# Second experts: eight places of 32 slots, weights of small places as whole rows, a new order of places

## The chip, the cores and the metric

The kernel runs on one core of one Trainium2 chip. The metric is the device time of one execution in microseconds (us). Each core has TensorE (PE; PEld is its weight load), VectorE (DVE), ScalarE (ACT), GpSimd (POOL) and SyncE (SP, which here only issues DMA), and 16 DMA engines.

## What is computed

Two transformer blocks run one after the other on 512 tokens of 1024 numbers, in float32. Each is a mixer and a mixture of experts. The change concerns the experts of the second block alone: 32 experts, of which a router picks 4 for every token. Cut to what matters:

```python
def moe_ffn(h, w_router, b_router, w_gu, b_gu, w_dn, b_dn):   # h: 512 x 1024
    logits = h @ w_router + b_router
    top_logits, top_e = lax.top_k(logits, 4)
    top_w = softmax(top_logits)
    ...                                    # tokens sorted by expert, blocks of one expert
    def expert_block(xe, e):
        gu = xe @ w_gu[e] + b_gu[e]        # 1024 -> 2048
        x_glu = minimum(gu[:, :1024], 7.0)
        x_lin = clip(gu[:, 1024:], -7.0, 7.0)
        act = (x_lin + 1) * (x_glu * sigmoid(1.702 * x_glu))
        return act @ w_dn[e] + b_dn[e]     # 1024 -> 1024
    ...                                    # y[token] += top_w * expert_block(...)
```

An expert's weights are 8 MiB for gate and up (w_gu, 1024 rows of 2048 numbers) and 4 MiB for down (w_dn): 12.58 MB, all of which are read for every expert that has a token. 512 x 4 = 2048 token-expert pairs are spread unevenly over the 32 experts.

## The kernel before

`moe2` (L2093) runs the second experts through `experts` (L1202), which lays out 32 **places**, one for each expert. Places 0 and 1 hold fixed experts; the others are filled on the chip by rank: `plan` (L838) sorts the experts by their number of tokens. Ranks are dealt to places by table: `PAIRS` names two places that have a second block of 64 slots beside 128 (a **pair**, for the two largest), and `SLOTS` names the places of 96 slots and of 64; all others have 128. Before, the places read, with A for 128 slots, M for 96, S for 64 and P for a pair: `AAASMSMSSMMSPSMSMSSMPMSASSSSSSSS`. The last eight are all S. A token that finds no slot is taken by `overflow` (L883), which counts extra blocks; they run in a loop behind the places (L1354), as often as that count says.

**Weights.** Every place takes 12 pieces of 1 MiB, in the order of the list `seq` (L1217): four gate/up pieces of the first half of the 1024 inner columns (hf = 0), the previous place's two down pieces of its second half, four gate/up pieces of hf = 1, two down pieces of hf = 0. A gate/up piece (`src_of`, L2105) is 128 partitions x 4 rows x 512 columns, so each partition reads four runs of 2 KB, and neighbouring partitions lie 64 KB apart. A down piece is 128 partitions x 2 rows x 1024 columns, one run of 8 KB a partition. Nine buffers (`wraw`, L97) hold them; SP issues the load of piece i when piece i - 9 has been used (`free`, L1296).

**Products.** Places of 128 and 96 slots, and pairs, split each weight piece into two parts (`split`, L112: `whi` on ACT L117, `wlo` on DVE L118) and take three products for each (`mm_block`); a pair puts the second block's work into the same stream. A place of 64 slots (`col`) multiplies the raw piece in fp32 with no split, and two such products of 64 rows stand **side by side** in one 128-row PSUM tile (`col_gu` L1031 for gate beside up, `col_dn` L1045 for the two halves of the 1024 output columns). The bias enters as one more product, of a selector `bsel` that POOL makes for each place (`bias_of`, L2121) with the table of biases. The activation (`act`, L1057 to 1080) works on one half at a time: `ea` and `eb` from PSUM, Silu on ACT, the multiply L1080 on DVE for a 64-slot place, on POOL otherwise; `act_turn` (L1084) transposes on TensorE into `pt`, and `act_split` (L1090) copies out `ah`.

**Lists and rows of tokens.** For each place POOL makes one-hots (`oh`, `list_hot` L926) from the plan; TensorE sums them up (`list_sum` L929, into `pt`), DVE turns the sum into indices (`list_end`), and POOL gathers the token rows (`x_gather` L992, `xg` from U) and at the end adds the weighted result to Y by an indirect DMA (`y_scatter`, L1128 to 1140, `eo`, whose operands come from ACT L1139 and DVE L1134).

**Order.** The program is in a hand-written order: step i of the loop at L1310 multiplies piece i of `seq`, and hooks put the other work at steps relative to that (`at`, `LEAD`): one-hots 17 steps ahead of a place's first piece, list sum 14, list end 13, gather 12, transposes of the tokens 4 and 2 steps ahead; act at 2 to 5 steps behind a half's last gate/up piece; the scatter 2 steps behind its last down piece. Each engine does its instructions in this order.

## Time and profile before

| what | us |
|---|---|
| time before, median of 3 runs (2493.81 to 2495.08) | 2494.42 |
| the profiled execution | 2502.25 |
| its span (first to last instruction) | 2500.4 |
| second experts in that span, from about | 1300 |
| to about | 2465 |
| busy in these 1165 us: TensorE | 1106.63 |
| DVE, ACT, POOL | 583.86, 450.06, 308.16 |
| moved there by DMA | 409.75 MB |

The mean granted TensorE clock of the profiled execution was 0.955 of full speed (2.4 GHz). How the views are read: a row of **windows** gives the window from:to in us, its length, then busy us and number of instructions of PE, PEld, DVE, ACT and POOL in that order, the granted TensorE clock (1 is full), the mean busy share of the 16 DMA engines (overlaps count, so it can exceed 1), and GB/s. A row of **waits** is: who waited, on what, then total us, times, longest. A row of **groups** is: line, engine, operation, out<-in with shapes and count | busy us, mean ns of one | idle of that engine just before, and what ended most of it. A row of the **timeline** is start us, duration us, engine, line, operation, and in brackets the idle time before it with its releaser.

### The profile page before, as it was taken

To read this page: it belongs to the slowest core of one execution; us is meant where nothing else is said; L and a number is where in the kernel's file an instruction comes from. 1 tells how busy PE (TensorE), PEld (TensorE's weight loads), DVE (VectorE), ACT (ScalarE), POOL (GpSimd) and SP (SyncE) were. 2 spreads that over 40 slices of the span, in tenths; PEclk is the share of its full clock that TensorE was granted. 3 is DMA by queue.
4 is the path that set the end of the run, shared out by engine and by line. 5 is a ranking of instruction groups with operands and counts; after the bars stand their busy time and mean duration, and the time that the engine had idled before them with its cause. 6 is when DMAs were issued, how large, how long until landed. Compare 5 with 4: busy or idle time off the path is not lost. (4 is left out here: it accounts for less than half of the span.)

```text
span 2500.4 us, 32116 instructions
## 1 busy us (share of the span) xinstructions
PE 2287.3 (91%) x11341; PEld 1447.2 (58%) x11341; DVE 1420.5 (57%) x2710; ACT 1051.0 (42%) x1605; POOL 593.7 (24%) x596
## 2 busy tenths in 40 slices
PE   6999977998978999999969999999999999998984
PEld 2655656774647886778747655455555467543331
DVE  5454698875638756544578655475456367531112
ACT  3333446865525445532347444354344256421001
POOL 2001134534313020000243222162322133131111
PEclk9999988999989999999979999999999999999997
DMA  8767538988976135223578999999799998999997
GB/s 283 234 201 245 177 127 320 378 305 304 335 265 180 57 80 159 60 89 93 185 286 298 336 390 381 392 357 339 254 360 389 381 336 257 324 379 391 389 394 229
DMA packets 264678, 683.78 MB, mean 273 GB/s; under 512 B 21260, under 2 KB 61028, under 8 KB 235840
## 3 DMA queue, kind: packets, MB, share of 16 engines
q1 hardware_dynamic: 240576, 607.88, 66.8%
q0 software_dynamic: 23648, 72.74, 11.0%
q8 instruction: 92, 1.51, 0.2%
q10 hardware_dynamic: 288, 1.05, 0.1%
q14 instruction: 74, 0.61, 0.1%
HBM read 643.74 MB, written 37.95 MB: 273 GB/s over the span
## 5 line engine op out<-in xcount | busy, mean ns | idle before, releaser
L118 DVE TENSOR_TENSOR wlo<-wraw,whi 128x1024 fp32r<-128x1024 f32 (+1 forms) x559 | 677.1, 1238 | 310.3 <-ACT whi L117 298.9
L117 ACT ACTIVATE whi<-wraw 128x1024 fp32r<-128x1024 f32 (+1 forms) x559 | 573.7, 1053 | 314.9 <-PE pm L80 120.8
L80 PE MATMUL pm<-wraw,xh 128*64 128x512 f32 x1280 | 321.9, 600 | 24.5 <-DMA wraw<-in_w_gu 24.3
L80 PE MATMUL pm<-whi,xh 128*128 128x512 f32 (+1 forms) x736 | 304.4, 414 | 3.4 <-ACT whi L117 3.4
L80 PE MATMUL pm<-wlo,xh 128*128 128x512 f32 (+1 forms) x736 | 291.7, 399 | 4.8 <-DVE wlo L118 4.8
L80 PE MATMUL pm<-whi,xl 128*128 128x512 f32 (+1 forms) x640 | 255.0, 399 | 0.0
L1140 POOL DMA_INDIRECT Y<-eo,isc x52 | 107.8, 2072 | 615.0 <-ACT eo L1139 232.4
L80 PEld LDWEIGHTS pm<-wraw,xh 128*64 128x64 f32 x1280 | 95.5, 137 | 208.2 <-issue 150.7
L1073 DVE TENSOR_SCALAR ea<-pm 64x512 f32<-64x512 f32 (+2 forms) x64 | 43.5, 680 | 235.1 <-PE pm L80 235.1
L80 PEld LDWEIGHTS pm<-whi,xh 128*128 128x128 f32 (+1 forms) x736 | 132.1, 179 | 59.7 <-issue 13.7
L80 PE MATMUL po<-wraw,ah 128*64 128x512 f32 x640 | 153.2, 601 | 0.1
L80 PEld LDWEIGHTS pm<-wlo,xh 128*128 128x128 f32 (+1 forms) x736 | 127.0, 172 | 41.0 <-DVE wlo L118 7.1
L992 POOL DMA_INDIRECT xg<-U,ig x52 | 88.6, 1704 | 226.4 <-issue 99.7
L926 POOL TENSOR_SCALAR oh<-slots,plan 128x64 bf16<-128x64 f32 (+2 forms) x168 | 139.1, 1051 | 0.4
L80 PEld LDWEIGHTS pm<-whi,xl 128*128 128x128 f32 (+1 forms) x640 | 113.8, 178 | 36.7 <-issue 0.6
L80 PE MATMUL po<-whi,ah 128*128 128x512 f32 (+1 forms) x320 | 132.5, 414 | 0.0
L80 PE MATMUL po<-whi,al 128*128 128x512 f32 (+1 forms) x320 | 128.1, 400 | 0.9 <-DVE al L1107 0.9
L80 PE MATMUL po<-wlo,ah 128*128 128x512 f32 (+1 forms) x320 | 128.2, 401 | 0.0
L1095 ACT ACTIVATE ah<-pt 128x256 f32<-128x256 f32 x40 | 15.4, 384 | 209.7 <-PE pt L1088 209.6
L1076 ACT ACTIVATE ea<-ea 64x512 f32<-64x512 f32 (+2 forms) x68 | 42.7, 628 | 140.7 <-DVE ea L1073 129.2
L80 PEld LDWEIGHTS po<-wraw,ah 128*64 128x64 f32 x640 | 51.3, 138 | 85.9 <-issue 80.1
L1080 POOL TENSOR_TENSOR eb<-eb,ea 96x512 f32<-96x512 f32 (+2 forms) x32 | 43.9, 1373 | 213.5 <-ACT ea L1076 153.5
(611 smaller groups left out, 4094.6 us busy)
## 6 DMA issues: line engine op xcount, KB each, us to landing
wraw<-in_w_gu SPq DMA_DIRECT2D x254, 1024.0 KB
wraw<-in_w_dn SPq DMA_DIRECT2D x127, 1024.0 KB
wraw<-in_w_e_down SPq DMA_DIRECT2D x32, 1024.0 KB
wraw<-in_w_e_up SPq DMA_DIRECT2D x31, 1024.0 KB
wraw<-in_w_e_gate SPq DMA_DIRECT2D x30, 1024.0 KB
wraw<-in_w_in SPq DMA_DIRECT2D x58, 512.0 KB
mz<-in_w_ada SPq DMA_DIRECT2D x80, 256.0 KB
wraw<-in_w_mod SPq DMA_DIRECT2D x26, 512.0 KB
```

Source lines behind the costliest of these rows:

```text
L80: self.nc.tensor.matmul(out, lhsT, rhs, start=start, stop=stop)
L117: nc.scalar.activation(h, v, AF.Copy)
L118: nc.vector.tensor_sub(l, v, h.bitcast(F32))
L926: (eng or self.nc.gpsimd).tensor_scalar(oh[:, c, :], self.slots[:, 0:n], poscol(c), None, op0=OP.is_equal)
L992: self.nc.gpsimd.indirect_dma_start(out=B.xg[0:B.n, :], out_offset=None, in_=self.U, in_offset=bass.IndirectOffsetOnAxis(ap=B.ig[:, :1], a ...
L1073: ve.tensor_scalar(a, g, 7.0, None, op0=OP.min)
L1076: nc.scalar.activation(a, a, AF.Silu, scale=1.702)
L1080: (nc.vector if B.col else nc.gpsimd).tensor_mul(B.b, B.b, B.a)
L1095: nc.scalar.activation(B.ah[hf], B.at.rearrange("p (k q) -> p k q", k=4), AF.Copy, scale=1.0 / 1.702 if B.bias else 1.0)
L1140: nc.gpsimd.indirect_dma_start(out=self.Y[:, :], out_offset=bass.IndirectOffsetOnAxis(ap=B.isc[:, :1], axis=0), in_=o, in_offset=None, com ...
```

## The change

Places of the second experts get a fourth size, and a new order: with X for 32 slots, `AAXMSMSPXXMSASMSPXXMSMSMXSMAXSSX`. There are 8 M, 10 S and 8 X (before 8 M and 18 S); the pairs stand at 7 and 16. In S and X places (**row** places)

- a gate/up piece is 128 partitions x 1 row x all 2048 columns: one run of 8 KB a partition, partitions 64 KB apart as before. `row_gu` multiplies gate and up of both halves from it; in an X place four products of 32 rows stand side by side in one PSUM tile (gate and up, two halves), in an S place two tiles hold two each (both halves of gate, both of up);
- both halves are activated at once (`row_act`, `row_turn`, `row_split`) on 2 x slots rows;
- all four down pieces follow behind the next place's first four gate/up pieces, so `seq` of a row place is eight gate/up pieces with the earlier place's four down pieces between the fourth and the fifth, and the scatter follows later. In an X place the down products stand four side by side too, and `y_scatter` adds two of them (ACT copy, then DVE multiply-add, for each half of the columns).

In all places the selector `bsel` has two halves of 128 rows (POOL: two operations of 128x128 for M, A and P where there was one, two of 128x64 for S and X as before for S), and the bias product goes over 128 rows. The first block's experts keep their tables and path.

```diff
-PAIRS = {2: (12, 20), 1: (6, 11)}
+PAIRS = {2: (7, 16), 1: (6, 11)}
...
+SLOTS = {2: ((3, 5, 10, 14, 19, 21, 23, 26),
+             (4, 6, 11, 13, 15, 20, 22, 25, 29, 30),
+             (2, 8, 9, 17, 18, 24, 28, 31)),
...
+    def row_gu(self, B, k, v):
+        n = B.n
+        if k == 0:
+            if B.col == 2:
+                B.pg = [self.pm.tile([128, 512], F32, name="pm") for _ in range(2)]
+            else:
+                p = self.pm.tile([128, 512], F32, name="pm")
+                B.pg = [p[0:64], p[64:128]]
+            for s in range(2):
+                for hf in range(2):
+                    B.bias("gu", B.pg[s][n * hf:n * hf + n], s, hf, True)
+        for s in range(2):
+            for hf in range(2):
+                c0 = 1024 * s + 512 * hf
+                self.mm(B.pg[s][n * hf:n * hf + n], B.xf[:, k, 0:n], v[:, 0, c0:c0 + 512], False, k == 7)
+    def row_dn(self, B, hf, jj, v):
+        n = B.n
+        if hf == 0 and jj == 0:
+            p = self.px.tile([128, 512], F32, name="po", tag="px")
+            B.po = [p[n * i:n * i + n] for i in range(B.col)]
+            for s in range(2):
+                B.bias("dn", B.po[s], s, 0, True)
+        for q in range(2):
+            for s in range(2):
+                i = s + 2 * q if B.col == 4 else s
+                self.mm(B.po[i], B.ah[hf][:, 2 * jj + q, :], v[:, q, 512 * s:512 * s + 512],
+                        hf == 0 and jj == 0 and i > 1, hf == 1 and jj == 1 and (q == 1 or B.col == 4))
+    def row_act(self, B, stage):
+        nc, ea, m = self.nc, self.ea, 2 * B.n
+        if stage == 0:
+            a = B.a = ea.tile([128, 512], F32, name="ea")[0:m]
+            b = B.b = ea.tile([128, 512], F32, name="eb")[0:m]
+            nc.vector.tensor_scalar(a, B.pg[0], 7.0, None, op0=OP.min)
+            nc.scalar.activation(a, a, AF.Silu, scale=1.702)
+            nc.vector.tensor_scalar(b, B.pg[1], 8.0, -6.0, op0=OP.min, op1=OP.max)
+        else:
+            nc.vector.tensor_mul(B.b, B.b, B.a)
+    def row_turn(self, B):
+        m = 2 * B.n
+        B.at = self.pt.tile([128, 512], F32, name="pt")[:, 0:4 * m]
+        for j in range(4):
+            self.nc.tensor.transpose(B.at[:, j * m:j * m + m], B.b[:, j:512:4], self.ident[0:m, 0:m])
+    def row_split(self, B):
+        m = 2 * B.n
+        ah = self.ea.tile([128, 4, 128], F32R, name="ah").bitcast(F32)[:, :, 0:m]
+        self.nc.scalar.activation(ah, B.at.rearrange("p (k q) -> p k q", k=4), AF.Copy, scale=1.0 / 1.702)
+        B.ah = [ah[:, :, 0:B.n], ah[:, :, B.n:m]]
...
-            (nc.vector if B.col else nc.gpsimd).tensor_mul(B.b, B.b, B.a)
+            nc.gpsimd.tensor_mul(B.b, B.b, B.a)
...
-            if B.col and s:
+            if B.col == 4:
+                nc.scalar.activation(d, B.po[s], AF.Copy, scale=B.w)
+                nc.vector.scalar_tensor_tensor(d, B.po[2 + s], B.w, d, op0=OP.mult, op1=OP.add)
+            elif B.col and s:
...
-        places = [[self.new_block(None, a > 0, 64 if a else size.get(b, 128), a > 0, size.get(b) == 64)
+        places = [[self.new_block(None, a > 0, 64 if a else size.get(b, 128), a > 0, {64: 2, 32: 4}.get(size.get(b), 0))
                    for a in range(2 if b in pairs else 1)] for b in range(E)]
+        rows = [nh == 2 and places[b][0].col > 0 for b in range(E)]
...
-                seq += [(b - 1, "dn", nh - 1, 0, jj) for jj in range(2)]
+                seq += [(b - 1, "dn", hf, 0, jj) for hf in range(0 if rows[b - 1] else nh - 1, nh) for jj in range(2)]
...
-                seq += [(b, "dn", 0, 0, jj) for jj in range(2)]
+                if not rows[b]:
+                    seq += [(b, "dn", 0, 0, jj) for jj in range(2)]
...
+            if rows[b]:
+                B, end = places[b][0], where[b, "gu", 1][-1]
+                for i, f in enumerate(((self.row_act, B, 0), (self.row_act, B, 1), (self.row_turn, B),
+                                       (self.row_split, B))):
+                    at(end + 1 if b == E - 1 else end + (1, 2, 4, 4.5)[i], *f)
+                at(where[b, "dn", 1][-1] + 2, self.y_scatter, B)
+                continue
...
+                    v = src[b]("row", 0, 0, 4 * hf + 2 * kk + s) if rows[b] else src[b]("gu", s, hf, kk)
+                raws[i] = self.raw(v, eng)
...
+                        if rows[b]:
+                            if q == 0 and what == "gu":
+                                self.row_gu(B, 4 * hf + 2 * kk + s, raws.pop(i))
+                            elif q == 0:
+                                self.row_dn(B, hf, s, raws.pop(i))
+                            else:
+                                free(i)
+                            continue
...
+                if what == "row":
+                    return w.rearrange("(p k) f -> p k f", k=8)[:, kk:kk + 1, :]
...
-        def bias_of(e, ef=None, col=False):
-            s_ = self.esm.tile([128, 128], F32R, name="bsel", bufs=4)
-            for d, v in ((s_[:, 0:64], ehalf[:, 0:1]), (s_[:, 64:128], ehalf[:, 1:2])) if col else ((s_, esel),):
-                nc.gpsimd.tensor_scalar(d, v.to_broadcast([128, d.shape[1]]), float(e) if ef is None else ef, None,
-                                        op0=OP.is_equal)
+        def bias_of(e, ef=None, col=0):
+            s_ = self.esm.tile([128, 2, 128], F32R, name="bsel", bufs=4)
+            for s in range(2):
+                nc.gpsimd.tensor_scalar(s_[:, s, 0:64 if col else 128],
+                                        ehalf[:, s:s + 1].to_broadcast([128, 64 if col else 128]),
+                                        float(e) if ef is None else ef, None, op0=OP.is_equal)
 
             def f(what, ps, s, hf, start):
-                c0, r = 512 * hf if what == "gu" else 1024, slice(64 * s, 64 * s + 64)
-                if col:
-                    self.mm(ps, s_[:, r].bitcast(F32), bias[:, c0:c0 + 512].bitcast(F32), start, False)
-                else:
-                    self.mm(ps, s_[r, 0:ps.shape[0]], bias[r, c0:c0 + 512], start, False)
+                c0 = 512 * hf if what == "gu" else 1024
+                l, r = s_[:, s, 0:ps.shape[0]], bias[:, c0:c0 + 512]
+                self.mm(ps, l.bitcast(F32) if col else l, r.bitcast(F32) if col else r, start, False)
```

The order on **PE at the end of the program**, where the last two places stand (there S and S, now S and X). `pm` are gate/up sums, `po` down sums, `xh` the tokens, `ah` the activated values, `wraw` the weight pieces; one row here is a run of equal instructions, a fp32 product counts once. Before, from the second half of place 30 on:

```order
L80 MATMUL po<-biasr,bsel 64x512 x2
L80 MATMUL po<-wraw,ah 64x512 x8
L80 MATMUL pm<-biasr,bsel 64x512 x2
L80 MATMUL pm<-wraw,xh 64x512 x8
L1088 MATMUL pt<-ident,eb 128x64 x4
L80 MATMUL pm<-wraw,xh 64x512 x8
L80 MATMUL po<-wraw,ah 64x512 x8
L80 MATMUL pm<-biasr,bsel 64x512 x2
L80 MATMUL pm<-wraw,xh 64x512 x8
L1088 MATMUL pt<-ident,eb 128x64 x4
L80 MATMUL pm<-wraw,xh 64x512 x8
L80 MATMUL po<-biasr,bsel 64x512 x2
```

Now, from the last gate/up products of place 30 (64 slots) to the end of place 31 (32 slots):

```order
L81 MATMUL pm<-wraw,xh 64x512 x8
L81 MATMUL pm<-biasr,bsel 32x512 x4
L81 MATMUL pm<-wraw,xh 32x512 x12
L1102 MATMUL pt<-ident,eb 128x128 x4
L81 MATMUL pm<-wraw,xh 32x512 x4
L81 MATMUL po<-biasr,bsel 64x512 x2
L81 MATMUL po<-wraw,ah 64x512 x16
L81 MATMUL pm<-wraw,xh 32x512 x16
L1102 MATMUL pt<-ident,eb 128x64 x4
L81 MATMUL po<-biasr,bsel 32x512 x2
L81 MATMUL po<-wraw,ah 32x512 x16
```

A place has one group of four transposes where it had two, its 16 down products stand in one row behind half of the next place's gate/up products, and in the last place they stand directly behind its transposes.

The order on **POOL in a 96-slot place that follows a 64-slot place**: `oh` are the one-hots, `eb` the multiply of the activation, `Y` the scatter of the place before, `xg` the gather. Before, at place 9:

```order
L1080 TENSOR_TENSOR eb<-eb,ea 96x512
L1140 DMA Y_114<-eo,isc 640x1024
L2124 TENSOR_SCALAR bsel<-ehalf,plan 128x64 x2
L926 TENSOR_SCALAR oh<-slots,plan 128x64 x4
L1080 TENSOR_TENSOR eb<-eb,ea 96x512
L992 DMA xg<-U_112,ig 64x1024
```

Now, at place 21:

```order
L1133 TENSOR_TENSOR eb<-eb,ea 96x512
L2204 TENSOR_SCALAR bsel<-ehalf,plan 128x128 x2
L927 TENSOR_SCALAR oh<-slots,plan 128x96 x4
L1196 DMA Y_114<-eo,isc 640x1024
L993 DMA xg<-U_112,ig 96x1024
L1133 TENSOR_TENSOR eb<-eb,ea 96x512
```

The scatter stands behind selector and one-hots now, where it stood ahead of them.

## Rows read from the trace of the kernel before

**Rows 1.** The page: busy time of each engine, share of the span, instructions.
```profile
PE 2287.3 (91%) x11341; PEld 1447.2 (58%) x11341; DVE 1420.5 (57%) x2710; ACT 1051.0 (42%) x1605; POOL 593.7 (24%) x596
```

**Rows 2.** Windows in the second experts: busy us (count), clock, DMA share, GB/s.
```profile
1300.00:2465.00 1165.00, 1106.63 (x4847) 604.24 (x4845) 583.86 (x787) 450.06 (x581) 308.16 (x286) 0.98 0.97 352
1300.00:1400.00 100.00, 94.53 (x419) 73.65 (x419) 82.19 (x92) 67.38 (x77) 43.33 (x32) 0.97 0.90 308
1425.00:1630.00 205.00, 196.35 (x869) 103.64 (x866) 111.96 (x165) 85.46 (x109) 45.78 (x44) 0.98 1.04 387
1630.00:1860.00 230.00, 220.38 (x963) 129.33 (x963) 132.24 (x172) 102.03 (x130) 83.35 (x64) 0.97 0.92 323
2020.00:2160.00 140.00, 138.44 (x592) 89.56 (x594) 86.99 (x99) 70.07 (x86) 40.41 (x35) 0.97 0.83 276
2261.00:2430.00 169.00, 150.31 (x640) 56.31 (x638) 27.42 (x59) 16.80 (x35) 21.64 (x33) 1.00 1.04 391
```

**Rows 3.** Windows cut at single places: 96 slots, 64, a pair, 64.
```profile
1646.00:1685.00 39.00, 39.00 (x178) 26.14 (x178) 33.07 (x43) 26.02 (x30) 26.97 (x16) 1.00 1.02 348
1685.00:1715.00 30.00, 30.00 (x145) 13.46 (x145) 12.29 (x17) 10.43 (x16) 4.01 (x7) 1.00 0.91 325
1715.00:1775.00 60.00, 60.00 (x255) 40.17 (x256) 32.90 (x41) 25.39 (x33) 20.64 (x16) 1.00 0.81 292
2295.00:2328.00 33.00, 29.69 (x129) 11.12 (x127) 5.64 (x13) 3.36 (x7) 4.95 (x8) 1.00 1.04 393
```

**Rows 4.** DMA view: 1300:2465, then 2306.5:2311 (2 KB), then 2369:2373.6 (mostly 8 KB).
```profile
DMA packets 153355, 409.75 MB, mean 352 GB/s; under 512 B 6962, under 2 KB 6962, under 8 KB 137330
DMA packets 873, 1.75 MB, mean 389 GB/s; under 512 B 25, under 2 KB 25, under 8 KB 871
DMA packets 345, 1.93 MB, mean 420 GB/s; under 512 B 28, under 2 KB 28, under 8 KB 136
```

**Rows 5.** Windows in the first experts, all weights in 8 KB runs.
```profile
440.00:460.00 20.00, 19.24 (x92) 15.52 (x91) 18.59 (x23) 16.23 (x19) 14.37 (x17) 1.00 1.01 400
460.00:480.00 20.00, 19.55 (x96) 15.52 (x95) 18.16 (x30) 16.75 (x23) 12.90 (x11) 1.00 1.03 359
```

**Rows 6.** Waits of TensorE, 1300 to 2465: total us, times, longest.
```profile
PE pm L80 <- DMA wraw<-in_w_gu: 24.3, 21, 2.2
PE pt L80 <- POOL oh L926: 20.9, 26, 4.8
```

**Rows 7.** Groups by shape, 1400 to 2500: busy us, mean ns, idle before.
```profile
L80 PE MATMUL pm<-wraw,xh 128*64 128x512 f32 x1152 | 290.9, 597 | 24.5 <-DMA wraw<-in_w_gu 24.3
L80 PE MATMUL po<-wraw,ah 128*64 128x512 f32 x576 | 138.3, 601 | 0.0
L1073 DVE TENSOR_SCALAR ea<-pm 64x512 f32<-64x512 f32 x36 | 24.5, 679 | 235.1 <-PE pm L80 235.1
L1080 DVE TENSOR_TENSOR eb<-eb,ea 64x512 f32<-64x512 f32 x36 | 24.5, 680 | 2.0
L2124 POOL TENSOR_SCALAR bsel<-esel,plan 128x128 fp32r<-128x128 f32 x10 | 15.5, 1551 | 0.1
```

**Rows 8.** Four 32-wide fp32 products, 960.9 to 962.2: tile view, then timeline.
```profile
L80 PE MATMUL pmod<-wraw,s x8: 592/604/617, 961.0 to 961.5; 128*32 128x512 f32 x8
961.01 1.07 PE L80 MATMUL pmod<-wraw,s 128*32 128x512 f32 x8
```

**Rows 9.** Timeline of POOL in a 96-slot place after a 64-slot place.
```profile
1627.22 4.48 POOL L1140 DMA_INDIRECT Y<-eo,isc  x1 [5.55 <-DVE eo L1134]
1631.23 3.91 POOL L2124 TENSOR_SCALAR bsel<-ehalf,plan 128x64 fp32r<-128x64 f32 x2
1635.12 2.50 POOL L926 TENSOR_SCALAR oh<-slots,plan 128x64 bf16<-128x64 f32 x4
```

**Rows 10.** Timeline at the end of the experts.
```profile
2465.44 0.68 ACT L1139 ACTIVATE eo<-po,slw 64x512 f32<-64x512 f32 x1 [4.59 <-PE po L80]
2466.16 0.75 DVE L1134 TENSOR_SCALAR eo<-po,slw 64x512 f32<-64x512 f32 x1 [7.03 <-ACTq L1354]
```

More of the change, by code (lines that the diff above doesn't have):

```diff
@@ L1042, in col_gu @@
             for s, v in enumerate((gv, uv)):
-                self.mm(B.pg[hf, s], B.xf[:, j, 0:64], v[:, k, :], j == 0 and not B.bias, j == 7)
+                self.mm(B.pg[hf, s], B.xf[:, j, 0:64], v[:, k, :], j == 0, j == 7)
     def col_dn(self, B, hf, jj, v, q, last):
@@ L1049, in col_dn @@
             B.po = [p[0:64], p[64:128]]
-            if B.bias:
-                for s in range(2):
-                    B.bias("dn", B.po[s], s, 0, True)
         for s in range(2):
             self.mm(B.po[s], B.ah[hf][:, j, :], v[:, q, 512 * s:512 * s + 512],
-                    j == 0 and hf == 0 and not B.bias, j == 3 and last)
+                    j == 0 and hf == 0, j == 3 and last)
+    def row_gu(self, B, k, v):
[13 more added lines that the diff above has]
+                self.mm(B.pg[s][n * hf:n * hf + n], B.xf[:, k, 0:n], v[:, 0, c0:c0 + 512], False, k == 7)
@@ L1095, in act_split @@
             nc.scalar.activation(B.ah[hf], B.at.rearrange("p (k q) -> p k q", k=4), AF.Copy,
-                                 scale=1.0 / 1.702 if B.bias else 1.0)
+                                 scale=1.0)
             return
```

10 lines of the change are left out of this document (4 added, 6 removed).

## The prediction

> **What bounds the kernel now.** All that changes lies in the second experts, 1300 to 2465 us of the span. Over the whole span the page has TensorE busiest, 91% [rows 1]; but the share is an average, so I read the windows of that stretch first [rows 2]: of 1165 us TensorE is busy 1106.6, and the DMA engines carry 409.75 MB at a share of 0.97. So both are near their limit, but not at the same moments. Where DMA runs at full rate the windows give 387 and 391 GB/s at a share of 1.04; in three other stretches they give 308, 323 and 276 GB/s. At 387 GB/s the 409.75 MB need 1059 us, so DMA stands idle for about 1165 - 1059 = 106 us, because all nine weight buffers are full and TensorE is behind. By the same division the stretch 1300:1400 holds 100 - 80 = 20 us of it (three 128-slot places), 1630:1860 holds 230 - 192 = 38 (places 9 to 12: 96, 96, 64, pair, with what stands behind them), and 2020:2160 holds 140 - 100 = 40 (places 19 to 22: 96, pair, 96, 64); 8 are elsewhere.
>
> The windows of single places [rows 3] say why. A 96-slot place holds TensorE busy for all of its 39 us, a pair for 60 us, a 64-slot place for 29.7 us, while DMA needs for the same places (12.58 MB of weights, and per slot 4 KB gathered and 4 KB scattered, at 387) 34.5, 36.6 and 33 us. So a 96-slot place costs 4.5 us more of TensorE than of DMA, a pair 23 more, a 64-slot place 3 less. The run of ten 64-slot places at the end is bound by DMA: 33 us for a place with TensorE at 29.69 [rows 3], 150 busy of 169 in the whole stretch [rows 2].
>
> The waits of TensorE [rows 6] show both bounds: 24.3 us for gate/up pieces (21 times), and 20.9 us for the one-hots that POOL makes. The timeline of POOL [rows 9] shows one case of the latter: the scatter of the previous place (4.48), two bias selectors (3.91) and four one-hots (2.50) in a row, and TensorE needs the last.
>
> **The change, part by part.** (1) *Whole rows.* In 18 small places (10 of 64 slots, 8 of 32) each of 8 gate/up pieces of 1.05 MB comes as one run of 8 KB per partition in place of four of 2 KB; the 4 down pieces have 8 KB runs already. The DMA view gives 389 GB/s where nearly all packets are of 2 KB, and 420 where most of the bytes come in 8 KB [rows 4]: 2.70 and 2.50 us for a piece. 144 pieces by 0.20 are **29 us** of DMA work. Nothing shows that this pattern reaches 420, so the bounds come from the first experts, whose weights all come in 8 KB runs: 400 GB/s in one window, 359 in the next, at shares of 1.01 and 1.03 [rows 5]. At 359 a piece takes 2.92, and 144 by 0.22 are 32 us lost. I take 420, because it is measured in the same stretch on the same queue, and keep both ends.
> The Trainium skill ("DMA: Bandwidth & Descriptors", section "Why small descriptors are slow") has a fixed cost of about 3 cycles beside one cycle per 32 bytes of a packet; by that 8 KB would save 3.4%, an estimate of 13 us for the 144 pieces in place of 29, and the sum would end at 2440. Rows 4 show 8%, so the sum goes by the rows.
>
> (2) *32 slots.* 8 places x 32 slots fewer are 256 x 8 KB = 2.1 MB: **5 us** of DMA. On TensorE, gate/up products of a 64-slot place take 290.9 / 18 = 16.2 us and down products 7.7 [rows 7], two side by side in 1.01 us. Four side by side stand elsewhere in the trace, in the second block's modulation: 8 instructions, four fp32 products, in 1.07 us, with 592 to 617 ns each [rows 8]. So 8 + 4 groups of four take some 12 us in place of 23.9, and with a third off the rest (bias, transposes) a 32-slot place takes TensorE about 16 us, DMA some 31. That is no gain by itself in a stretch where DMA sets the pace; what it gives is that TensorE catches up after a slow run.
>
> (3) *Both halves activated at once.* DVE does three operations of 679 to 680 ns on one 128-row tile in place of six on 64 rows [rows 7], 2 us per place, and TensorE 4 transposes instead of 8: I put a 64-slot place at 29 us. DVE is off the path there (5.64 of 33 us busy [rows 3]): nothing beyond the 0.7 us of TensorE, which part 4 counts. The act now begins only when all gate/up pieces are through, and the next place's first four pieces are multiplied meanwhile; only the last place has nothing behind it. There the order goes from gate/up straight into act, transposes and 16 down products. Its chain is longer by about 1.4 us (two DVE steps after the ACT step of 0.68, at 0.75 [rows 10]) and TensorE's own work after the last piece shorter by about 1.5: nothing.
>
> (4) *New order of places.* A place is named here by its slots. With the costs above (64 slots now 29 and 31.4, since 33 - 8 x 0.2) I look for runs in which TensorE needs more than DMA. Places 3 to 7 (96, 64, 96, 64, pair): TensorE 2 x 39 + 2 x 29 + 60 = 196, DMA 2 x 34.5 + 2 x 31.4 + 36.6 = 168: 28 us. Places 10 to 16 (96, 64, 128, 64, 96, 64, pair, a 128 at 39 and 35.2): 264 against 235: 29. Places 19 to 23 and 26, 27 gain 4 or 5 on DMA at a time and are followed by a 32-slot place: 5 together. The start has two places of 128 before a small one instead of three: 15 for 20. For comparison the same sum for the old runs (96, 96, 64, pair: 168 against 139, and the other likewise) gives 29 each, where 38 and 40 were idle; the 10 on top are the POOL waits [rows 6], and the nine buffers, which at 2.6 us a piece could in the best case take up 24 us of each, took up nothing that is seen. Now both pair runs come behind 32-slot places, from which TensorE comes with its buffers emptied, so I take off 3 or 4 each: 25 + 25 + 5 + 15 = **70 idle** in place of 106, a gain of 36. The bounds: 103 idle (all waits stay) to 40 (the buffers take up most of both runs).
>
> (5) *POOL.* The bias selector costs a second 128x128 operation in the 14 big places, 14 x 1.55 = 22 us [rows 7], and the multiply of the act leaves DVE there as before. POOL is busy 308 of 1165 us [rows 2], so that has room, except in front of a one-hot. The new order puts the one-hots of a 96-slot place ahead of the scatter before it, and the 4.48 us of that scatter [rows 9] fall out of the wait, while 2 to 3 us of selector come in. I count nothing beyond what part 4 says. On SP the down pieces are issued later by four gate/up pieces; SP issues in order of use, so nothing is queued behind a wait that wasn't.
>
> The sum: 29 + 5 + 36 = 70 us. The profiled execution took 2502.25 us, a span of 2500.4; less 70 is 2432. The median of the runs shown, 2494.42, lies 7.8 below it: **2424 us**.
>
> **The rivals.** *The POOL waits stay or move* to the gathers: 103 idle, gain 34 + 3, 2457 us. For it: selectors got longer [rows 7, 9]. Against: the scatter is gone from in front. Chance 0.15. *Rows land no faster*: 29 lost, 2453; for it the 359 in the first experts [rows 5]; 0.11. Both together 2486; 0.02. *The buffers take up the pair runs*: 40 idle, gain 34 + 66, 2394; for it the 32-slot places ahead of both runs; 0.13. *Four products don't run side by side* where they write the same tile that is read next, or the granted clock falls, as TensorE is idle half of such a place: TensorE then needs 29 to 32 as for 64 slots, it doesn't catch up, 5 to 10 us, 2429 to 2434; against it [rows 8] and a granted clock of 0.97 to 1.00, the level of 2.4 GHz, in all windows [rows 2]; 0.04.
> *Slower: the pitch.* One 8 KB run of each partition, 64 KB apart, in place of four runs of 2 KB with the same pitch, may fall on the same part of memory. The gain of 70 is gone when a row piece takes 2.50 + 70 / 144 = 2.99 us (351 GB/s), and beyond that the change is slower; at twice a 2 KB piece, 5.4 us, the time is 2424 + 144 x 2.9 = 2842. At the slowest that a saturated window shows, 359 [rows 5], it is 2485. Against it: the 2 KB pieces have the same pitch and run at 389 [rows 4]. Chance 0.03.
> The Trainium skill (the same page, "Latency and other measured facts") has such a rule: copies with a row pitch of 512 KiB between partitions ran at 207 GB/s. By that, as an estimate, a piece would take 5.1 us and the time would be 2424 + 144 x 2.6 = 2798. The trace speaks against it so far: 389 at a pitch of 64 KB.
> *An expert overflows*: the eight 32-slot places have no room for a 33rd token, and one more block after the loop costs at least the weights again (33 us, rows 3) with nothing beside them, so some 2424 + 60 to 100, about 2500. Counted on the reference, the largest of the last eight experts has exactly 32 tokens, the 64-slot ones at most 62; it fits unless rounding in the router tips one token. Chance 0.02.
>
> **How the numbers follow.** The forecast has 0.50, its own range 2405 to 2445 (the store of buffers by 15 us, the row rate between 400 and 420). With the rivals at 2394, 2429, 2453 and 2457 the range is 2390 to 2460. A measurement of this kernel tells about 0.2% (5 us) from no change. Slower by more than that: the pitch beyond 2.99 us, and the overflow, 0.05. Within 0.2%: what is between, 0.02. Faster: 0.93.
>
> **What would show it.** In the profile after: single row pieces at 2.5 us and a DMA view near 410 GB/s in the tail (if 389, the second rival); 64-slot places of some 31.5 us there; two stretches of low DMA share, one that ends with place 7 and one with place 16, about 25 us each (40 in all: buffers; 35 and more each: POOL); TensorE some 16 us busy in a 32-slot place, and the wait for one-hots down from 20.9 to about 10. A granted clock near the 1.2 GHz level in 32-slot places, a block behind the loop, or pieces of 3 us would make the prediction wrong.

## The result and the profile after

The changed kernel takes 2410.73 us (median of 4 runs, 2409.51 to 2412.66), the kernel before in the same measurement 2494.11 us (4 runs): a ratio of 0.9668, 95% interval 0.9652 to 0.9685. That is 83 us less, where 70 were forecast; 2410.73 lies inside the forecast's range (2390 to 2460) and inside its own narrower one (2405 to 2445).

The profiled execution took 2409.98 us, its span 2408.2. How much of that lies in the second experts is read from a mark that only they have, the first bias product. The view of the tile `biasr`, before and after: shortest, median and longest ns, then first and last start in us.

```profile
L80 PE MATMUL pm<-biasr,bsel x212: 437/592/792, 1278.5 to 2444.0; 128*64 128x512 f32 x72, 64*128 64x512 f32 x16, 64*96 64x512 f32 x16, 64*64 64x512 f32 x2
L81 PE MATMUL pm<-biasr,bsel x212: 389/592/774, 1261.8 to 2332.8; 128*64 128x512 f32 x42, 128*32 128x512 f32 x32, 128*128 128x512 f32 x16, 128*96 128x512 f32 x16
```

From there to the end of the span are 2500.4 - 1278.5 = 1221.9 us before and 2408.2 - 1261.8 = 1146.4 after: **75.5 us** come from the second experts. The other 16.7 of the 92 us between the two profiled executions lie ahead of them, where the products and the loads are the same. The profiled execution of before is 7.8 us above its median; if all of that lies ahead of the mark, some 8 of the measured 83 us are not the change's by any step named here. In the other kernels below the mark stands between 1260.2 and 1272.5, with the same code ahead of it, so it moves by more than these 8 us without any change; one of them has the code of before throughout and only another order, and its mark is at 1265.4.

Windows of after, with the columns of [rows 2]: the stretch that answers to 1300:2465, its start, then first pair, the two 32-slot places behind it, the places between, second pair, the places behind it, and the end.

```profile
1283.00:2374.00 1091.00, 983.58 (x4771) 559.53 (x4769) 546.89 (x742) 436.12 (x552) 393.04 (x297) 0.95 0.98 374
1283.00:1383.00 100.00, 88.09 (x437) 63.35 (x439) 64.51 (x79) 53.33 (x64) 46.36 (x33) 0.93 0.87 307
1499.00:1562.00 63.00, 63.00 (x281) 43.46 (x285) 35.13 (x44) 25.41 (x33) 26.80 (x23) 0.97 0.85 328
1562.00:1630.00 68.00, 50.10 (x297) 24.94 (x290) 27.16 (x60) 18.04 (x27) 13.78 (x11) 0.85 0.98 365
1630.00:1820.00 190.00, 183.24 (x852) 105.08 (x850) 109.12 (x142) 89.54 (x110) 80.51 (x58) 0.98 1.03 396
1820.00:1882.00 62.00, 62.00 (x273) 43.13 (x272) 33.28 (x42) 24.36 (x32) 26.27 (x22) 0.97 0.83 319
1882.00:1950.00 68.00, 49.02 (x295) 23.91 (x294) 22.52 (x36) 17.52 (x25) 15.62 (x13) 0.85 0.96 363
2285.00:2370.00 85.00, 63.19 (x322) 18.53 (x318) 10.05 (x19) 7.28 (x14) 5.16 (x4) 0.94 1.01 414
```

The DMA view of the same stretch and of its end, where 64- and 32-slot places stand in a row (to compare with [rows 4]):

```profile
DMA packets 97588, 407.84 MB, mean 374 GB/s; under 512 B 6963, under 2 KB 6963, under 8 KB 63123
DMA packets 5002, 35.22 MB, mean 414 GB/s; under 512 B 589, under 2 KB 589, under 8 KB 820
```

TensorE's waits (compare [rows 6]), and the groups of products in small places, 10 of 64 slots and 8 of 32 (compare [rows 7]):

```profile
PE pt L81 <- POOL oh L927: 36.1, 35, 5.0
PE pt L1005 <- DMA xg<-U,ig: 21.9, 2, 11.2
PE pm L81 <- DMA wraw<-in_w_gu: 14.9, 16, 2.6
PE po L81 <- DMA wraw<-in_w_dn: 13.6, 15, 1.4
PE pt L1141 <- POOL eb L1133: 11.4, 4, 5.5
```

```profile
L81 PE MATMUL pm<-wraw,xh 128*64 128x512 f32 x640 | 148.6, 603 | 5.0 <-DMA wraw<-in_w_gu 5.0
L81 PE MATMUL po<-wraw,ah 128*64 128x512 f32 x320 | 72.0, 595 | 3.5 <-DMA wraw<-in_w_dn 3.5
L81 PE MATMUL pm<-wraw,xh 128*32 128x512 f32 x512 | 66.1, 627 | 9.9 <-DMA wraw<-in_w_gu 9.9
L81 PE MATMUL po<-wraw,ah 128*32 128x512 f32 x256 | 39.3, 621 | 10.4 <-DMA wraw<-in_w_dn 10.1 <-SPq L1432 0.2
```

By the forecast's own division: the full rate is now 396 GB/s (1630:1820), so 407.84 MB need 1030 us of 1091, and DMA is idle for 61 us where it was 106. The start holds 100 - 77.5 = 22 of it, the pairs with what stands behind them 11 + 5 = 16 and 12 + 6 = 18, the rest 5. TensorE's busy time, 1106.63 before, is 983.58.

The mean clock of these windows hides something. In a place of 32 slots TensorE had no work for 10.69 us (the row stands under "Why the prediction was right"); the next window has a granted clock of 0.50, the level of 1.2 GHz, and in it 16 product instructions of this place take nearly twice as long as the next 16 do, when the clock has risen:

```profile
1604.00:1609.00 5.00, 4.54 (x21) 1.34 (x22) 2.05 (x3) 1.73 (x3) 0.00 (x0) 0.50 1.02 393
1605.29 3.64 PE L81 MATMUL pm<-wraw,xh 128*32 128x512 f32 x16
1609.49 1.92 PE L81 MATMUL pm<-wraw,xh 128*32 128x512 f32 x16
```

So a wait of TensorE can cost more than its own length. As an estimate, TensorE's busy time by the missing share of the clock, added up in windows of 2 us from the mark to 40 us before the end, is 20 us in the kernel before, 37 in the changed one, and 24 in the kernel with early one-hots below. How much of that is on the path isn't shown.

### The profile page after: what moved, and what is told of

It reads as the page before. It is cut to its first block, busy times and chain, and to the rows that moved or that the text cites. A ratio compares the mean times of both kernels' runs of the same rounds, so it can differ in the third digit from the quotient of the medians.

```text
span 2408.2 us, 31803 instructions
## 1 busy us (share of the span) xinstructions
PE 2150.7 (89%) x11269; PEld 1395.7 (58%) x11269; DVE 1383.2 (57%) x2666; ACT 1037.6 (43%) x1577; POOL 681.6 (28%) x610
## 3 DMA queue, kind: packets, MB, share of 16 engines
q0 software_dynamic: 23136, 70.64, 10.7%
## 5 line engine op out<-in xcount | busy, mean ns | idle before, releaser
L81 PE MATMUL pm<-wlo,xh 128*128 128x512 f32 (+1 forms) x736 | 297.5, 407 | 1.3 <-DVE wlo L119 1.2
L81 PE MATMUL pm<-wraw,xh 128*64 128x512 f32 (+1 forms) x1280 | 245.1, 614 | 14.9 <-DMA wraw<-in_w_gu 14.9
L927 POOL TENSOR_SCALAR oh<-slots,plan 128x64 bf16<-128x64 f32 (+3 forms) x168 | 157.4, 1045 | 0.3
L81 PEld LDWEIGHTS pm<-wraw,xh 128*64 128x64 f32 (+1 forms) x1280 | 65.8, 128 | 141.0 <-issue 108.3
L81 PE MATMUL po<-wraw,ah 128*64 128x512 f32 (+1 forms) x640 | 126.1, 606 | 14.0 <-DMA wraw<-in_w_dn 13.6
L1005 PEld LDWEIGHTS pt<-ident,xg 64*128 64x128 f32 (+3 forms) x416 | 57.3, 197 | 80.2 <-DMA xg<-U,ig 34.4
L1005 PE MATMUL pt<-ident,xg 64*128 64x64 f32 (+3 forms) x416 | 69.6, 291 | 38.2 <-DMA xg<-U,ig 36.6
L1016 DVE TENSOR_TENSOR xl<-pt,xh 128x512 fp32r<-128x512 f32 (+1 forms) x52 | 32.5, 625 | 122.2 <-ACT xh L1014 122.0
L1014 ACT ACTIVATE xh<-pt 128x512 fp32r<-128x512 f32 (+2 forms) x60 | 31.3, 522 | 147.0 <-PE pt L1005 138.0
L81 PEld LDWEIGHTS po<-wraw,ah 128*64 128x64 f32 (+1 forms) x640 | 35.7, 127 | 90.9 <-issue 60.7
```

Source lines behind the costliest of these rows:

```text
L81: self.nc.tensor.matmul(out, lhsT, rhs, start=start, stop=stop)
L927: (eng or self.nc.gpsimd).tensor_scalar(oh[:, c, :], self.slots[:, 0:n], poscol(c), None, op0=OP.is_equal)
L1005: self.nc.tensor.transpose(B.xt[:, k * n:k * n + n], B.xg[0:n, 4 * h2 + k:1024:8], self.ident[0:n, 0:n])
L1014: nc.scalar.activation(B.xh[:, d, 0:n], pv, AF.Copy)
L1016: nc.vector.tensor_sub(lo, pv, B.xh[:, d, 0:n].bitcast(F32))
```

## The experiments

All ratios are to the kernel before, run on the same chip beside each; where two kernels are compared, the difference of their ratios is meant, in us of the kernel before, unless the text says medians. The last column is the profiled time from the first bias product to the end of the span, as above.

| kernel | median us | ratio, 95% interval | us from the mark |
|---|---|---|---|
| before | 2494.11 | 1 | 1221.9 |
| after | 2410.73 | 0.9668 (0.9652 to 0.9685) | 1146.4 |
| e1_2kb | 2422.37 | 0.9736 (0.9707 to 0.9765) | 1149.8 |
| e1b_4kb | 2404.61 | 0.9659 (0.9635 to 0.9682) | 1140.6 |
| e2_x64 | 2428.90 | 0.9750 (0.9723 to 0.9777) | 1160.4 |
| e3_oldorder | 2466.32 | 0.9909 (0.9883 to 0.9935) | 1190.2 |
| e4_before_order | 2464.02 | 0.9894 (0.9867 to 0.9920) | 1196.4 |
| e5_onehots_early | 2399.64 | 0.9637 (0.9611 to 0.9662) | 1130.5 |
| e6_pair_between | 2415.58 | 0.9697 (0.9669 to 0.9724) | 1144.7 |
| e7_8buffers | 2410.07 | 0.9681 (0.9653 to 0.9708) | 1138.5 |
| e8_old_selector | 2439.73 | 0.9814 (0.9779 to 0.9848) | 1167.9 |
| e9_pair_between_early | 2395.29 | 0.9619 (0.9588 to 0.9649) | 1125.0 |
| e10_early_old_selector | 2409.55 | 0.9678 (0.9649 to 0.9707) | 1138.9 |
| e11_early_64rows | 2411.09 | 0.9666 (0.9647 to 0.9686) | 1139.9 |

### Parts alone and parts undone

**Old order under the new code, and new order under the old code.** The theory was that the terms of the sum stand by themselves and add up; the rivals were that faster loads only turn into idle time, and that the order pays only with the rest. The first edit puts the old tables into the changed kernel:

```diff
-PAIRS = {2: (7, 16), 1: (6, 11)}
+PAIRS = {2: (12, 20), 1: (6, 11)}
...
-SLOTS = {2: ((3, 5, 10, 14, 19, 21, 23, 26), (4, 6, 11, 13, ...), (2, 8, 9, ...)),
+SLOTS = {2: ((4, 6, 9, 10, 14, 16, 19, 21), (3, 5, 7, 8, 11, ...)),
```

> The changed kernel with the tables of the kernel before (old order, 18 places of 64 slots, none of 32): row loads and the joint activation alone. Theory: 18 x 8 pieces by 0.2 us off, the idle of the old runs stays or grows a little: 2465 to 2472 us, a gain of 22 to 29 on the kernel before. Rival (faster loads only turn into more idle in runs where TensorE is behind): above 2480 us. Rival (rows are the main gain): below 2450 us.

Measured: 0.9909, some 23 us faster than the kernel before, as the theory had it. The second edit puts the new order into the kernel before, its 32-slot places as places of 64:

```diff
-PAIRS = {2: (12, 20), 1: (6, 11)}
+PAIRS = {2: (7, 16), 1: (6, 11)}
...
-SLOTS = {2: ((4, 6, 9, 10, 14, 16, 19, 21), (3, 5, 7, 8, 11, ...)),
+SLOTS = {2: ((3, 5, 10, 14, 19, 21, 23, 26), (2, 4, 6, 8, 9, 11, ...)),
```

> The kernel before with only the new order of places (its 32-slot places as 64-slot ones, old loads, old activation). Theory (the terms add up: 62 us of the joint-64 kernel less 17 to 23 for the rows): some 40 us faster than the kernel before, 2450 to 2460 us. Rival (the order pays only together with faster loads or with 32-slot places, since it is TensorE's surplus that counts): within 15 us of the kernel before, above 2478 us.

Measured: 0.9894, some 26 us faster; less than the theory's 40, more than the rival's 15.

**32 slots as 64.** In the changed kernel:

```diff
-             (4, 6, 11, 13, 15, 20, 22, 25, 29, 30),
-             (2, 8, 9, 17, 18, 24, 28, 31)),
+             (2, 4, 6, 8, 9, 11, 13, 15, 17, 18, 20, 22, 24, 25, 28, 29, 30, 31)),
```

> The changed kernel with its eight 32-slot places as 64-slot places in the same order. Theory: 5 us more DMA work and about 10 us more idle DMA around the pairs, because TensorE catches up less (29 us a place against 16): 2425 to 2432 us. Rival (32 slots matter only by their bytes): 2416 us. Rival (they carry most of the gain): above 2450 us.

Measured: 2428.90, 0.9750, inside the theory's 2425 to 2432. So 32 slots are worth some 20 us (14 from the mark), of which 5 are bytes. This kernel has the new code and the new order with 18 places of 64 slots, and closes a square: code alone 23, order alone 26, both 62. By the ratios they are worth 13 us more together than apart, but each ratio has an interval of some 6 us to either side, and by the marks (31.7, 25.5 and 61.5) it is 4 us: that they help each other at all is likely, the size isn't shown. Where the code helps in the new order can be seen. Both kernels of the new order are level up to the first pair, whose first down bias product starts at 1564 in either; the next 96-slot place, two 64-slot places later, has its own at 1675 with the old code and at 1665 with the new. The windows of that stretch, old code, then new:

```profile
1564.00:1675.00 111.00, 103.90 (x461) 52.74 (x461) 50.18 (x89) 36.47 (x51) 28.59 (x28) 0.98 0.89 317
```

```profile
1564.00:1665.00 101.00, 98.61 (x456) 50.98 (x454) 46.29 (x76) 34.39 (x45) 29.29 (x30) 1.00 0.87 326
```

It is bound by TensorE (103.90 of 111 us busy, 98.61 of 101), and DMA at 317 and 326 GB/s is not full. Of the 10 us, 5.3 are TensorE's own work (some 2 of them, as an estimate, the granted clock of 0.98 against 1.00), the rest its gaps (7.1 to 2.4), mostly waits for one-hots. Behind the second pair the same stretch takes 110 and 101 us. So in these two stretches the new code gains where TensorE is the bound and DMA is not full: there its cheaper small places and bias products and its fewer waits count, not its loads. In the old order the like stretches (from the down products of place 12 to those of 14, and of 20 to those of 21) take 82.2 and 49.9 us with the old code, 82.5 and 46.6 with the new; they hold one 64-slot place and none in place of two. There the new code gains nothing and 3 us behind the pairs. So what it gains there depends on the order, while over all places together the marks leave 4 us of that.

**Rows cut.** In the changed kernel every row piece is loaded in two transfers, of two 2 KB runs or of one 4 KB run per partition:

```diff
+        if isinstance(src, list):
+            for hh in range(2):
+                d = t[:, 1024 * hh:1024 * hh + 1024].rearrange("p (s c) -> p s c", s=2)
+                (eng or self.nc.sync).dma_start(d, src[hh])
...
-                c0 = 1024 * s + 512 * hf
+                c0 = 1024 * hf + 512 * s          # 2 KB runs only
```

> The changed kernel, only that a whole row is loaded as two transfers of two 2 KB runs per partition (columns permuted in the buffer, products the same). Theory (the gain is made of row loads 29 us, fewer slots 5, less idle DMA 36 to 50): 144 pieces by 0.2 us, about 29 us slower than the changed kernel, 2440 us; packets of 2 KB near 389 GB/s. Rival (order and 32-slot places do it all, run length doesn't matter where DMA isn't saturated): 2411 us. Rival (rows give more than their 29, since the share of time with DMA saturated has grown): 2450 or more.

> Control of the former: two transfers for a row piece as there, but each of one 4 KB run per partition. If run length is what counts, this lies between, nearer to the changed kernel: 2412 to 2425 us. If it is the second transfer and its issue that costs, it is as slow as the 2 KB kernel.

Measured: 0.9736 and 0.9659. Between the two only the run length differs: 0.0077, 19 us (18 in the medians), though just 9 from the mark. The DMA view of the last 60 us of places, and TensorE's wait for one-hots, first with 2 KB, then with 4 KB:

```profile
DMA packets 9495, 23.43 MB, mean 390 GB/s; under 512 B 658, under 2 KB 658, under 8 KB 8677
PE pt L81 <- POOL oh L932: 6.7, 12, 3.7
```

```profile
DMA packets 5598, 24.48 MB, mean 408 GB/s; under 512 B 652, under 2 KB 652, under 8 KB 4571
PE pt L81 <- POOL oh L932: 7.7, 12, 3.7
```

390 and 408 GB/s, where whole rows gave 414 (415 in the same 60 us of the changed kernel). The two kernels differ in the run length alone, so that is the cause, and 4 KB bring most of it. Against the changed kernel the 2 KB version loses 17 us and not 29, but it has 6.7 us of waits for one-hots and not 36.1; beside the kernel below that has none (0.9637), it loses 25, and the 4 KB version 5. Rows are worth 17 to 25 us by this; by the marks 3 (against the changed kernel) to 19 (against the one below). As an estimate from the two rates, 144 pieces at 414 GB/s in place of 390 are 22 us where DMA sets the pace all the time. The 23 us under the old order are those of the whole new code, bias products and joint activation with them.

### The waits for one-hots

The forecast had them go down from 20.9 to about 10; they rose to 36.1. So I took them away:

```diff
-                at(s0 - lead[0] - o, prep, b, B)
+                at(s0 - lead[0] - o - (3 if nh == 2 and b > 3 else 0), prep, b, B)
```

> The changed kernel with selector and one-hots of every place from the fifth on issued three steps earlier. Its waits of TensorE for one-hots (36.1 us in 35 times there) should fall to under 10. Theory (outside of the runs at the two pairs DMA sets the pace, and these waits lie beside it): the time stays within 5 us, 2403 to 2411 us. Rival (these waits are on the path): 20 to 30 us off, below 2392 us.

Measured: 2399.64, 0.9637, and no wait for one-hots made by POOL among the rows. 36 us of waits were worth 11 by the medians, 8 by the ratios (whose intervals overlap) and 16 from the mark: more than the theory's 5, less than the rival's 20. Part of it need not be the waits themselves, but the lower clock behind them. What made them so long, groups of POOL suggest: first of after, then of this kernel (the one-hots of 64-slot places, and the multiply of the activation), and last the multiply of before:

```profile
L927 POOL TENSOR_SCALAR oh<-slots,plan 128x64 bf16<-128x64 f32 x40 | 42.4, 1292 | 0.0
L1133 POOL TENSOR_TENSOR eb<-eb,ea 96x512 f32<-96x512 f32 x16 | 40.1, 2503 | 47.8 <-DVE eb L1128 38.0 <-ACT ea L1129 9.8
```

```profile
L927 POOL TENSOR_SCALAR oh<-slots,plan 128x64 bf16<-128x64 f32 x40 | 17.5, 453 | 0.0
L1133 POOL TENSOR_TENSOR eb<-eb,ea 96x512 f32<-96x512 f32 x16 | 20.4, 1276 | 12.1 <-DVE slsb L941 7.0 <-ACT ea L1129 3.4 <-DVE eb L1128 1.7
```

```profile
L1080 POOL TENSOR_TENSOR eb<-eb,ea 96x512 f32<-96x512 f32 x16 | 21.3, 1331 | 110.7 <-ACT ea L1076 85.8 <-DVE eb L1075 15.1 <-DVE slsb L940 7.5
```

The same one-hot takes 1292 ns or 453, the same multiply 2503 or 1276. In the kernel before the multiply took 1331, and one-hots were slow there too (942 for 64 slots). The timeline of DVE and of POOL in after has one such multiply, and one that is free:

```profile
2024.97 6.89 DVE L119 TENSOR_TENSOR wlo<-wraw,whi 128x1024 fp32r<-128x1024 f32 x6
2025.21 7.78 POOL L1133 TENSOR_TENSOR eb<-eb,ea 96x512 f32<-96x512 f32 x1 [6.67 <-DVE eb L1128]
2047.92 1.30 POOL L1133 TENSOR_TENSOR eb<-eb,ea 96x512 f32<-96x512 f32 x1 [0.50 <-ACT ea L1129]
```

The multiply that is issued at 2025.21 ends at 2032.99, 1.1 us after DVE has ended a row of six weight splits (2024.97 to 2031.86); 23 us later the same multiply takes 1.30. Three multiplies of the changed kernel take 7.75 to 7.78 us, and each begins within 0.3 us of the start of such a row of six splits. So it is held as long as the whole row lasts. The Trainium skill ("SBUF — State Buffer", section "SBUF: two separate sides") says that DVE and GpSimd share one pair of ports under an exclusive lock, which a DVE operation with two SBUF inputs takes for the whole instruction; the trace agrees, with 7.78 us against 1.30, and shows in addition that six such instructions in a row hold it for all six. POOL's work is priced by where it falls beside DVE, then, and a new order moves it. That this is all of the growth from 20.9 to 36.1 isn't shown: the kernel with each pair between two 32-slot places, below, has 39.0 us of these waits with the same multiply at 1672 ns on the mean.

**POOL's second selector undone.** The forecast priced it at nothing beyond the waits. The edit makes one operation for a big place and lets the bias product read 64 of its rows, as before:

```diff
-            for s in range(2):
+            for s in range(2 if col else 1):
+                v = ehalf[:, s:s + 1] if col else esel
...
+                if not col:
+                    h = slice(64 * s, 64 * s + 64)
+                    self.mm(ps, s_[h, 0, 0:ps.shape[0]], bias[h, c0:c0 + 512], start, False)
+                    return
```

> The changed kernel with the selector of the kernel before in the 14 big places: one POOL operation of 128x128 and bias products over 64 rows. POOL loses 14 operations of about 1.55 us, 22 us. Theory (POOL's selector stands ahead of one-hots that TensorE waits for, and where TensorE is the bound, that is in the runs with the pairs, the wait is on the path; taking all of those waits away by earlier one-hots gave 11 us): 3 to 8 us faster than the changed kernel, 2403 to 2408 us, waits for one-hots down from 36 to 15 to 25. Rival (as the prediction had it, the second operation costs nothing): 2411 us.

> Earlier one-hots and the selector of the kernel before, together, in the order of the changed kernel. Theory (both remove the same waits): no more than 3 us below the kernel with earlier one-hots alone, 2396 to 2400 us. Rival (POOL's time counts elsewhere too, in front of gathers and the activation of the pairs): below 2394 us.

Both went the other way. In the changed kernel the old selector costs 0.0146, some 36 us (21 from the mark); with earlier one-hots 0.0041, some 10 (8 from the mark). Rows of the former: the multiply on POOL, and TensorE's waits.

```profile
L1133 POOL TENSOR_TENSOR eb<-eb,ea 96x512 f32<-96x512 f32 x16 | 50.5, 3156 | 52.5 <-DVE eb L1128 42.6 <-ACT ea L1129 9.9
PE pt L81 <- POOL oh L927: 30.3, 33, 4.4
PE pt L1141 <- POOL eb L1133: 15.4, 5, 5.2
```

The multiply is up to 3156 ns, held by splits more often. But TensorE waits only 4 us longer for it than in the changed kernel (15.4 against 11.4), and 6 us less for one-hots, so the waits don't explain the loss; with early one-hots the wait for the multiply is 5 us with either selector. Some 8 us more than with early one-hots are lost in the stretch behind the first pair, where TensorE is busy 86.81 of 109 us at a clock of 0.86 (1557:1666), against 82.38 of 101 at 0.90 in the changed kernel (1551:1652); what sets that off stays open. The 10 us that are lost with early one-hots too must be in the other half of the edit, if POOL's lighter work costs nothing.

**The bias product over 64 rows alone.** Earlier one-hots, two selector operations as in the changed kernel, and only the rows that the product reads cut:

```diff
-                l, r = s_[:, s, 0:ps.shape[0]], bias[:, c0:c0 + 512]
+                h = slice(0, 128) if col else slice(64 * s, 64 * s + 64)
+                l, r = s_[h, s, 0:ps.shape[0]], bias[h, c0:c0 + 512]
```

> Earlier one-hots, POOL's two selector operations as in the changed kernel, but the bias products of the big places over 64 rows (the half of the selector that holds ones) instead of 128. It parts the two halves of the former kernel's edit. Theory (a 64-row product between 128-row ones holds TensorE up, some 0.73 us from the product before it to the one behind it against 0.47 in the changed kernel): as slow as earlier one-hots with the old selector, 2405 to 2412 us, a ratio of about 0.967 to the kernel before. Rival (it was POOL's work or the code's place, not TensorE): 2398 to 2402 us, a ratio of 0.9635.

Measured: 0.9666 (0.9647 to 0.9686) against 0.9637 (0.9611 to 0.9662), 7 us, and 9.4 us from the mark: the theory's number. The intervals overlap by a little; the profile decides. TensorE does the same products from the mark to the down products of the last place, but is busy 17 us longer (early one-hots alone, then this kernel):

```profile
1267.30:2358.00 1090.70, 992.75 (x4834) 560.81 (x4832) 554.96 (x759) 446.48 (x566) 309.84 (x310) 0.96 0.99 380
1269.40:2366.90 1097.50, 1010.05 (x4835) 556.14 (x4834) 555.86 (x757) 448.37 (x566) 308.10 (x310) 0.96 0.99 378
```

Its timeline in this kernel, and at the like place in after:

```profile
2030.07 0.40 PE L81 MATMUL pm<-whi,xl 128*96 128x512 f32 x1
2030.39 0.47 PE L81 MATMUL pm<-biasr,bsel 64*96 64x512 f32 x1
2030.79 0.47 PE L81 MATMUL pm<-whi,xh 128*96 128x512 f32 x1
2031.10 0.39 PE L81 MATMUL pm<-wlo,xh 128*96 128x512 f32 x1
```

```profile
2036.36 0.40 PE L81 MATMUL pm<-whi,xl 128*96 128x512 f32 x1
2036.59 0.40 PE L81 MATMUL pm<-biasr,bsel 128*96 128x512 f32 x1
2036.83 0.40 PE L81 MATMUL pm<-whi,xh 128*96 128x512 f32 x1
2037.06 0.39 PE L81 MATMUL pm<-wlo,xh 128*96 128x512 f32 x1
```

Products follow each other every 0.23 us. Around one of 64 rows the steps are 0.32, 0.40 and 0.31, together 1.03 us from the product before it to the second behind it; around one of 128 rows 0.23, 0.24 and 0.23, 0.70 us. So here a change between 128 and 64 rows and back costs 0.33 us. By the groups view there are 54 such products into gate/up sums of 96 and 128 columns in the stretch; at 0.33 each they are 18 us of TensorE, as an estimate, and 17 are measured. About half of it shows in the time, since TensorE is the bound for part of the time only. The Trainium skill ("TensorEngine Tiling (Array Packing)", "Key Properties") says that changing the tiling mode drains TensorE; the trace agrees, with these 0.33 us.

### Order and buffers

> The changed kernel with eight weight buffers in place of nine. Theory (the buffers take up part of each run in which TensorE is behind, about 2.6 us a piece, at three places: start and two pairs): 5 to 10 us slower than the changed kernel, 2416 to 2421 us. Rival (the store takes up nothing, as in the sum of the prediction): 2411 us. Rival (fewer transfers in flight cost rate everywhere): above 2430 us.

The edit is the number of buffers (9 to 8) and the list of their places. Measured: 0.9681, no difference from the changed kernel. This doesn't settle what the ninth buffer is worth: this kernel has 10.7 us of waits for one-hots against 36.1; at the 8 to 16 us for 36 of the run with early one-hots that is worth some 6 to 11, as much as the theory had the buffer lose.

> The changed kernel with another order of the same places: AAXMSMSSMXPXASMSMXSMSMSXPXAMXSSX, in which each pair stands between two 32-slot places, so that no run has TensorE behind DMA by more than the nine buffers take up. Theory: the idle DMA at the pairs goes from about 18 to about 8 each by what a pair alone costs (23 us of TensorE more than DMA, a store of up to 24 for it); with the surplus of the 128-slot place behind it 5 to 15 us off, 2396 to 2406 us. Rival (the run's length doesn't count, only the pair): 2411 us, no change.

The edit is `PAIRS` at 10 and 24 and `SLOTS` for that string. Measured: 0.9697, no gain. The row of its waits:

```profile
PE pt L81 <- POOL oh L927: 39.0, 24, 10.0
```

39 us, one of 10.0. With these taken away as above:

> Earlier one-hots and the order with each pair between two 32-slot places, together. Theory (that order lost its gain to waits for one-hots, 39 us with one of 10.0, at other places): these waits fall under 10 and it ends 5 to 12 us below the kernel with earlier one-hots alone, 2388 to 2395 us. Rival (a pair costs the same wherever it stands): 2397 to 2402 us.

Measured: 2395.29, 0.9619 (0.9588 to 0.9649), the fastest of all. Beside 0.9637 (0.9611 to 0.9662) it is 4 us better in the medians and 5.5 from the mark, at the edge of the theory's range, and the intervals overlap: that the order helps isn't shown. Its window and what TensorE waits for now:

```profile
1285.00:2376.00 1091.00, 987.16 (x4809) 554.85 (x4808) 550.53 (x752) 439.87 (x562) 306.67 (x300) 0.97 0.99 378
PE pm L81 <- DMA wraw<-in_w_gu: 25.3, 24, 2.8
PE po L81 <- DMA wraw<-in_w_dn: 12.8, 16, 1.4
```

378 GB/s over the whole stretch, and the longest waits are for weights. By the forecast's division (412.57 MB at 396 GB/s, 1042 us) DMA is still idle for some 49 of these 1091 us.

## Why the prediction was right

It named what bounds each stretch, and the total was short by 13 us of 83. In its own two terms, DMA's work gave 29 us where 34 were forecast and the idle time 45 where 36 were, so errors of both signs met in the total, and that it is as near as this is in part luck. By its terms:

- **DMA work.** Forecast 1059 to 1025 us, measured 1030. Rows of 8 KB land nearly as fast as forecast (414 GB/s at the end, by which a piece takes 2.53 us where 2.50 were forecast), but the term of 29 us is worth 17 to 25 by the ratios. Neither the pitch nor a slow row shows in these 414 GB/s. The 13 us that the prediction estimated from the Trainium skill ("DMA: Bandwidth & Descriptors", section "Why small descriptors are slow") are less than the ratios show.
- **32 slots.** Forecast 5 us of bytes and a catch-up inside the idle term; measured 20 by the ratios, 14 from the mark. Four products stand side by side: (66.1 + 39.3) / 8 = 13.2 us of TensorE where 12 were forecast, against (148.6 + 72.0) / 10 = 22.1 for 64 slots.
- **Idle DMA.** Forecast 70, measured 61: pairs 16 and 18 instead of 25 each, the start 22 instead of 15, the rest 5 as forecast. One slip is in the forecast's sum: by its own formula a 64-slot place needs 33.9 us of DMA at 387 GB/s and not 33, which makes the two runs together some 4 us too high. That the buffers took up more of the runs than the 3 or 4 us that were taken off is the likely rest; it isn't shown. The 34 us of the two pairs lie midway between the forecast's 50 and the 20 that the rival of the buffers leaves them.
- **The waits for one-hots** were the wrong step in part 5: they rose, as the first rival had it, but without its price: of 36 us, 8 to 16 show in the time. POOL's operations were priced by their own length, while those that meet a row of DVE's splits last as long as the row.
- **What was left out:** the bias product over 128 rows, described in the change and priced nowhere, is worth some 7 to 9 us. That is more than the forecast of the second experts lacks (75.5 against 70).
- **The granted clock.** A clock near the 1.2 GHz level in 32-slot places was to be a sign against the prediction. It came, 0.50 in 1604:1609, in the second 32-slot place behind a pair, behind the 10.69 us in which TensorE had nothing to do. The forecast held all the same, and DMA ran at 393 GB/s and a share of 1.02 in these 5 us. The rival that named this fall, and TensorE's idle time as its cause, priced it at 5 to 10 us; no such loss is shown.
- **A new wait** that the forecast didn't have; no price of it is shown. In the second 32-slot place behind a pair TensorE waits for the gather, twice, 21.9 us in all. The rows of POOL, then of TensorE:

```profile
1579.04 1.49 POOL L1196 DMA_INDIRECT Y<-eo,isc  x1 [17.14 <-DVE eo L1193]
1590.06 1.60 POOL L1196 DMA_INDIRECT Y<-eo,isc  x1 [9.53 <-DMA Y<-eo,isc]
1591.96 0.97 POOL L993 DMA_INDIRECT xg<-U,ig  x1 [0.30 <-issue]
1604.45 0.91 PE L1005 MATMUL pt<-ident,xg 96*128 96x96 f32 x4 [10.69 <-DMA xg<-U,ig]
```

POOL's scatter waits 9.53 us for the one before it to land, and the gather stands behind it. The window 1562:1630 has a DMA share of 0.98 meanwhile, and in a 32-slot place TensorE has time: it is busy 50 of 68 us. But DMA falls short of its full rate by 5 and 6 us in these two windows, by the division above, and the kernel with each pair between two 32-slot places and early one-hots, the fastest, doesn't have this wait. That its cost is small is argued, not measured.

About 8 us of the gain lie ahead of the second experts by this count and stay unexplained; that is no more than the mark moves between kernels.

## What to carry to other kernels

Where two engines are each the bound for part of the time, count for each stretch what either needs, and put the cheap work where the one that is behind can catch up: order alone and the new code alone gave 26 and 23 us here, both together 62, with 4 to 13 of these from the two together. When a rewrite also changes a detail of a hot stream (here the rows that a bias product reads), price it per instruction as well, since 0.33 us a time was worth as much as a named part. A wait that grows isn't yet a loss, and one that is taken away isn't yet a gain: 36 us of waits were worth 8 to 16. And a mean clock over a long window hides the stretches at half speed behind each long wait.

## What the runs showed of the hardware

- A POOL operation of 1.3 us took 7.8 where DVE had six splits of two SBUF operands in a row beside it (6.89 us); it got no turn between them.
- A product over 64 rows between products over 128 cost 0.33 us more than one over 128 rows with zeros in the other half (1.03 against 0.70 us over three steps).
- Runs of 4 KB loaded nearly as fast as runs of 8 KB (408 and 414 GB/s), runs of 2 KB at 390, in the same stretch of the kernel.
- Behind 10.69 us without work the granted clock stood at 0.50, the level of 1.2 GHz, and 16 product instructions took 3.64 us where the next 16 took 1.92.
